# An up-projection by seven block products per tile, in fixed slots, behind two plain tiles

## The chip, the cores and the metric

The kernel runs on one core of one Trainium2 chip. Its time is the device time of one execution in microseconds (us). Before the change the median of three runs is 2341.06 us (2338.14 to 2341.59). The engines are TensorE (PE, with PEld for its weight loads), VectorE (DVE), ScalarE (ACT), GpSimd (POOL) and SyncE (SP, which issues the DMAs here).

## The reference

One layer of a hybrid backbone: a mixer (a recurrent branch and a state-space branch, merged), then a gated MLP with a 3x3 depthwise convolution on a 16 x 64 grid of 1024 tokens, each with its norm, modulation and residual. The change lies in the MLP, with D_MODEL 1024 and FFN_DIM 2816:

```python
def conv_ffn(h, w_up, conv_w, conv_b, w_down, rows, cols):
    u, v = jnp.split(h @ w_up, 2, axis=-1)
    u = dwconv2d(u, conv_w, conv_b, rows, cols)
    return (jax.nn.gelu(u) * v) @ w_down
...
        hx2 = modulate(rmsnorm(x, norm_ffn_w[l]), mx[3], mx[4])
        x = x + mx[5] * conv_ffn(hx2, ffn_w_up[l], ffn_conv_w[l], ffn_conv_b[l], ffn_w_down[l], rows, GRID_W)
```

## The kernel before

Activations lie with features on the 128 partitions and the 1024 tokens along the columns (T = 1024, half H = 512). Every fp32 product is done in three matmuls: an operand is split into a high part (ACT copies it to a rounded type) and a low part (DVE subtracts the copy), and `gdense` adds hi*hi, hi*lo and lo*hi over the K tiles of 128 features, 512 columns at a time, with `matmul` on line 124. Weights come by `wload`: a DMA into `raw` (512 KB), then the split into `whi`/`wlo`, with two of each, at high priority. The small helpers `stt`, `tt` and `act` (lines 156, 159, 162) issue all DVE and ACT work, so these three lines appear in most rows.

`tail` runs the MLP. `wout` writes the mixer's result into x1 (tiles M0 to M7) for the first and then the second half of the tokens. The norm of a half (`norm`, then `apply` per K tile: DVE scales, ACT writes the high part, DVE the low part, into tiles A0 to A15) is woven into what follows: the norm of the second half into the first up tile. Then `up` runs for f = 0 to 21. One tile f is 128 features of u and of v: 2 x 8 x 3 x 2 = 96 matmuls of 512 columns, u into a PSUM tile `d`, v into two PSUM tiles `s`. On u follow the convolution (ACT: centre tap and bias, `facc<-d,vec`; DVE: eight taps, `facc<-d,vec,facc`), the gelu on ACT, the product with v on DVE (`facc<-facc,s`), and the split into a pair of H tiles. After f = 7 and f = 14 `down` multiplies seven of these h tiles by the down weights, eight output tiles by two halves, and adds into x1; after f = 21 `last_down` does the last eight h tiles in pieces of 512, 256 and 256 tokens, with the final norm of a piece woven into the next one.

The order on each engine in this stage is left to the tile scheduler: by priority and readiness, with the program's order as its first guide. The tiles H, A, M, `raw` and `facc` rotate in pools, so a tile comes free when its last reader is done.

Of the kernel before, what the change touches and what calls it, by code (L numbers as in the profile page):

```python
# [45 lines left out]
class Builder:  # L46
    def __init__(self, nc, tc, A):
        self.nc, self.tc, self.A = nc, tc, A
        self.uid = 0
        self.wslot = 0  # L50
        self.groom = False
        self.turn = False
        self.wx = None
        self.st = getattr(nc, self.STORE)
# [100 lines left out]
    def stt(self, out, in0, s, in1, op0=ALU.mult, op1=ALU.add):  # L155
        self.nc.vector.scalar_tensor_tensor(out, in0, s, in1, op0=op0, op1=op1)  # L156

    def tt(self, out, a, b, op=ALU.mult):
        self.nc.vector.tensor_tensor(out, a, b, op=op)  # L159

    def act(self, out, in_, f, **kw):
        self.nc.scalar.activation(out, in_, f, **kw)  # L162
# [107 lines left out]
    def setup(self, cpool):  # L270
# [6 lines left out]
        self.mU = self.t(cpool, P, "mU")  # L277
        self.mL = self.t(cpool, P, "mL")
# [3 lines left out]
        nc.gpsimd.affine_select(out=self.mU, in_=self.ones, pattern=[[1, P]], compare_op=ALU.is_ge,  # L282
                                fill=0.0, base=0, channel_multiplier=-1)
        nc.gpsimd.affine_select(out=self.mL, in_=self.ones, pattern=[[-1, P]], compare_op=ALU.is_ge,
                                fill=0.0, base=0, channel_multiplier=1)
# [406 lines left out]
    def ssd(self):  # L692
# [429 lines left out]
    def up(self, f, x, split, parts):  # L1122
        A, p2, fh, fl = self.A, self.p2, x["fh"], x["fl"]
        pu = self.t(self.psD, T, "d")
        spans = [[(0, H)], [(H, T)]] if split else [self.FULL]
        wu = self.wload(A["wup"][f])
        if split:
            wv = self.wload(A["wup"][NF + f])
            pv = [self.t(self.psS, H, "s") for _ in range(2)]
            for sp in spans[:1]:  # L1130
                yield from self.gdense(pu, wu, fh, fl, sp)
                yield from self.gdense(pv, wv, fh, fl, sp)
            spans = spans[1:]
        for sp in spans:
            yield from self.gdense(pu, wu, fh, fl, sp)
        acc = self.t(p2, T, "facc")
        wc = [self.v("ffn_conv_w", tap * NF + f) for tap in range(9)]
        a3 = acc.rearrange("p (r c) -> p r c", c=64)
        u3 = pu.rearrange("p (r c) -> p r c", c=64)
        step = 16 // parts  # L1140
        for q in range(parts):
            lo, hi = q * step, q * step + step
            self.act(a3[:, lo:hi], u3[:, lo:hi], AF.Identity, bias=self.v("ffn_conv_b", f), scale=wc[4])
            for tap in (1, 7, 0, 2, 3, 5, 6, 8):
                dy, dx = tap // 3 - 1, tap % 3 - 1
                r0, r1 = max(lo, -dy), min(hi, 16 - max(0, dy))
                c0, c1 = max(0, -dx), 64 - max(0, dx)
                o = a3[:, r0:r1, c0:c1]
                self.stt(o, u3[:, r0 + dy : r1 + dy, c0 + dx : c1 + dx], wc[tap], o)
        if not split:  # L1150
            wv = self.wload(A["wup"][NF + f])
            pv = [self.t(self.psS, H, "s") for _ in range(2)]
        for sp in spans:
            yield from self.gdense(pv, wv, fh, fl, sp)
        i = f % 8
        h = self.t(self.pH, T, f"H{2 * i}", F32R)
        l = self.t(self.pH, T, f"H{2 * i + 1}", F32R)
        step = T // parts
        for q in range(parts):
            sl = slice(q * step, q * step + step)  # L1160
# [191 lines left out]
```

## Time and profile before

| | us |
|---|---|
| median of 3 runs | 2341.06 |
| the profiled execution | 2342.84 |
| its span, first to last instruction | 2341.1 |
| TensorE busy (matmuls) | 2285.2 (98%) |
| DVE busy | 1613.5 (69%) |
| ACT busy | 1061.3 (45%) |
| POOL busy | 2.4 (0%) |
| mean granted TensorE clock | 0.99 |

A row of the profile names line, engine and operation, then out<-in by the names that the program gives its tiles, shapes, and how many. "Idle before" tells how long the engine had stood still and what released it. The first up tile starts near 1604 us, the last one ends near 2235 us.

### The profile page before, as it was taken

How to read it: one execution, taken by the hardware profiler on the slowest of the kernel's cores; microseconds unless marked ns; L12 is line 12 of the kernel's file. 1: busy time of each engine (PE TensorE's matmuls, PEld its weight loads, DVE VectorE, ACT ScalarE, POOL GpSimd, SP SyncE). 2: the span in 40 equal slices, each digit the busy share in tenths (PEclk: the TensorE clock that was granted, in tenths of full speed). 3: DMA queues.
4: the chain of work that ended last, by engine and by line, in shares of the span. 5: the costliest groups of instructions: out<-in, count | busy, mean ns of one | idle time of the engine just before them, and what ended most of it. 6: DMA issues, size and time to landing. Idle time of an engine off the chain costs nothing.

```text
span 2341.1 us, 29454 instructions
## 1 busy us (share of the span) xinstructions
PE 2285.2 (98%) x11530; PEld 1896.3 (81%) x11530; DVE 1613.5 (69%) x2586; ACT 1061.3 (45%) x1596; POOL 2.4 (0%) x14
## 2 busy tenths in 40 slices
PE   7999999999999999999999999999999999999998
PEld 3778878778888888888888778888888888888888
DVE  4977877889978858758866675467764367436655
ACT  4477667677766556656635222333221122112231
POOL 0000000000000000000000000000000000000000
PEclk8999999999999999999999999999999999999999
DMA  6212222144434334424348765432111111111112
GB/s 253 95 62 73 95 84 70 59 129 149 133 124 149 120 102 142 145 77 150 114 136 271 233 220 187 154 97 63 54 44 48 53 45 52 42 51 54 46 54 73
DMA packets 81455, 251.78 MB, mean 108 GB/s; under 512 B 9731, under 2 KB 15907, under 8 KB 76069
## 3 DMA queue, kind: packets, MB, share of 16 engines
q1 hardware_dynamic: 81312, 249.90, 32.9%
q8 instruction: 90, 1.47, 0.3%
q14 instruction: 49, 0.39, 0.1%
q10 hardware_dynamic: 4, 0.01, 0.0%
HBM read 222.33 MB, written 27.54 MB: 107 GB/s over the span
## 4 chain that ended last, share of the span: by engine, by line
PE 84%; DVE 10%; DMA 3%; ACT 2%; issue 1%; DVEq 0%; ACTq 0%
PE d L124 42%; PE s L124 30%; PE s L985 2%; PE s L656 2%; PE s L977 1%; DVE wlo L159 1%; DVE L L159 1%; PE s L926 1%; DMA adar<-in_ada 1%; PE s L925 1%; ACT L L162 1%; PE s L314 1%; DVE L L681 1%; DMA raw<-in_w 1%; PE s L598 1%
## 5 line engine op out<-in xcount | busy, mean ns | idle before, releaser
L124 PE MATMUL d<-H,whi 128*128 128x512 f32 x2464 | 690.4, 398 | 0.4 <-ACT whi L162 0.2
L124 PEld LDWEIGHTS d<-H,whi 128*128 128x128 f32 x2464 | 451.0, 189 | 93.5 <-issue 6.0
L162 ACT ACTIVATE whi<-raw 128x1024 fp32r<-128x1024 f32 (+1 forms) x194 | 203.1, 1049 | 567.3 <-PE s L124 346.5
L124 PE MATMUL d<-H,wlo 128*128 128x512 f32 x1232 | 386.5, 393 | 2.0 <-DVE wlo L159 2.0
L159 DVE TENSOR_TENSOR wlo<-raw,whi 128x1024 fp32r<-128x1024 f32 (+1 forms) x194 | 234.4, 1210 | 188.7 <-ACT whi L162 187.2
L124 PEld LDWEIGHTS d<-H,wlo 128*128 128x128 f32 x1232 | 229.9, 188 | 51.5 <-DVE wlo L159 3.7
L124 PE MATMUL s<-A,whi 128*128 128x512 f32 x960 | 258.4, 389 | 0.0
L124 PE MATMUL d<-A,whi 128*128 128x512 f32 x960 | 258.3, 389 | 0.0
L124 PE MATMUL s<-H,whi 128*128 128x512 f32 x832 | 252.5, 391 | 2.7 <-ACT whi L162 2.7
L156 DVE SCALAR_TENSOR_TENSOR facc<-d,vec,facc 128x945 f32<-128x945 f32 (+5 forms) x184 | 216.8, 1178 | 11.2 <-ACT facc L162 5.9
L124 PEld LDWEIGHTS d<-A,whi 128*128 128x128 f32 x960 | 180.2, 188 | 37.6
L124 PEld LDWEIGHTS s<-A,whi 128*128 128x128 f32 x960 | 180.2, 188 | 37.3
L124 PEld LDWEIGHTS s<-H,whi 128*128 128x128 f32 x832 | 156.6, 189 | 36.0 <-ACT whi L162 3.1
L162 ACT ACT_TABLE_LOAD x102 | 130.9, 1283 | 84.3 <-DVE cacc L156 28.9
L156 DVE SCALAR_TENSOR_TENSOR M<-s,mods,M 128x512 f32<-128x512 f32 (+1 forms) x72 | 49.7, 691 | 160.4 <-PE s L124 160.2
L124 PE MATMUL s<-H,wlo 128*128 128x512 f32 x416 | 157.4, 391 | 1.4 <-DVE wlo L159 1.3
L124 PE MATMUL s<-A,wlo 128*128 128x512 f32 x480 | 149.2, 389 | 0.5 <-DVE wlo L159 0.5
L124 PE MATMUL d<-A,wlo 128*128 128x512 f32 x480 | 149.1, 389 | 0.0
L124 PEld LDWEIGHTS s<-A,wlo 128*128 128x128 f32 x480 | 90.0, 188 | 19.5 <-DVE wlo L159 1.0
L124 PEld LDWEIGHTS d<-A,wlo 128*128 128x128 f32 x480 | 90.1, 188 | 18.7
L156 DVE SCALAR_TENSOR_TENSOR E<-E,cst 128x128 f32<-128x128 f32 x256 | 82.3, 349 | 19.5 <-ACT E L162 19.5
L162 ACT ACTIVATE m<-GU,dtt 128x128 f32<-128x128 f32 x256 | 78.7, 389 | 35.0 <-PE s L977 29.8
(273 smaller groups left out, 3130.4 us busy)
## 6 DMA issues: line engine op xcount, KB each, us to landing
raw<-in_w SPq DMA_DIRECT2D x92, 512.0 KB, 3.6
E<-csd SPq DMA_DIRECT2D x32, 1024.0 KB, 6.7
raw<-in_wup SPq DMA_DIRECT2D x44, 512.0 KB, 3.6
R<-csd SPq DMA_DIRECT2D x64, 256.0 KB, 4.6
adar<-in_ada SPq DMA_DIRECT2D x32, 512.0 KB, 3.9
gated<-sg SPq DMA_DIRECT2D x32, 256.0 KB, 3.8
gd<-y SPq DMA_DIRECT2D x32, 256.0 KB, 2.3
gk<-gd SPq DMA_DIRECT2D x32, 256.0 KB, 5.6
```

The source lines that it names most:

```text
L124: nc.tensor.matmul(o, a[:, k, :], b[k][:, xo + s : xo + e], start=(k == 0 and i == 0), stop=(k == kn - 1 and i == 2))
L156: self.nc.vector.scalar_tensor_tensor(out, in0, s, in1, op0=op0, op1=op1)
L159: self.nc.vector.tensor_tensor(out, a, b, op=op)
L162: self.nc.scalar.activation(out, in_, f, **kw)
L314: self.nc.tensor.matmul(ps[:2, :], scc[:, k, :], w[:, k, :], start=(k == 0), stop=(k == 7))
L598: nc.tensor.matmul(pss, self.bt[j // 4][:, c, :], xw[:, c, :, :], start=(c == 0), stop=(c == 1))
L656: nc.tensor.matmul(pg, a[:, q, :], b[:, s:e], start=(i == 0), stop=(i == 2))
L681: nc.vector.tensor_tensor_scan(b1[:, L - 1 : TX - 1 : -1], a[:, L - 1 : TX - 1 : -1], b1[:, L - 1 : TX - 1 : -1], b1[:, 0:1], op0=ALU.mult ...
L925: nc.tensor.matmul(ps[:, s - s2, 0, :], btok[:, s, :], xw[:, 0, s, :], start=True, stop=True)
L926: nc.tensor.matmul(ps[:, s - s2, 1, :], btok[:, 7 - s, :], xw[:, 1, 7 - s, :], start=True, stop=True)
L977: nc.tensor.matmul(psy[q, c, :], self.xt[:, c0 + c, q], m[:, h, c, :], start=True, stop=True)
L985: nc.tensor.matmul(pso[:, c, :], S[:, cc if d == 0 else 7 - cc, d, :], CT[:, cc * P : (cc + 1) * P], start=True, stop=True)
```

## The change

Tiles f = 0 and 1 are kept plain (`up_plain`): the same 96 matmuls, written as eight products of a half of K by a half of the tokens. For f = 2 to 21 the tile is a 2 x 2 block product (K halves; u and v; token halves) that is done by a Winograd form with seven products instead of eight. The blocks of the activations are added and subtracted once (`blocks` during tiles 0 and 1: 24 DVE and 12 ACT operations; `blocks_late` in slots 2 to 9: the fourth block of product 22, 16 DVE and 4 ACT). The blocks of the weights are added per tile on POOL (`up_sum` and inside `up_split`, four per tile), and POOL also makes the low part of each of the seven weight blocks. Sums of products are formed in PSUM where the sign allows it, and three partial sums per tile are copied out by ACT and added back by DVE.

`ups` sets the order: one slot per product (4 K tiles x 3 = 12 matmuls), with the weight split three slots ahead, two taps of the previous tile's convolution per slot in four slots, the gelu in the next and the two gate products in the one after. All instructions of these slots are pinned to the program's order on every engine (`pin`). Product 22 of a tile is done one tile later, in the second slot. Since the A and H tiles hold the blocks, the gated h tiles are stored to DRAM (`h_d`) and loaded again (`hload`) for the down rounds, which now all run after the last up tile. The masks mU and mL are made later, when the state-space stage opens.

The instructions by engine: PE loses 240 matmuls of 128x512 and nothing else; DVE goes from 2588 to 2635 and ACT from 1600 to 1785; POOL gets 220 two-input operations of 128x512 and four of 128x1024; SP gets 22 stores to and 22 loads from `hd`. Ahead of the tail the order is the same on every engine, but for mU and mL on POOL.

```diff
 
     def stt(self, out, in0, s, in1, op0=ALU.mult, op1=ALU.add):
-        self.nc.vector.scalar_tensor_tensor(out, in0, s, in1, op0=op0, op1=op1)
+        self.pin(self.nc.vector.scalar_tensor_tensor(out, in0, s, in1, op0=op0, op1=op1))
...
-        self.mU = self.t(cpool, P, "mU")
-        self.mL = self.t(cpool, P, "mL")
...
+            self.mU = self.t(q1, P, "mU")
+            self.mL = self.t(q1, P, "mL")
...
+    PRODUCTS = ("11", "12", "s2", "s1", "s3", "s4", "22")
+    CLASSIC = 2
+    AHEAD_SPLIT = 3
+
+    def pin(self, ins):
+
+        return self.tc.keep_in_program_order(ins) if self.pinned else ins
+
+    def ptt(self, out, a, b, op):
+        self.pin(self.nc.gpsimd.tensor_tensor(out, a, b, op=op))
+
+    def up_plain(self, f, x, split):
+
...
+        for n, hf in ((0, 0), (1, 0), (0, 1), (1, 1)) if split else ((0, 0), (0, 1), (1, 0), (1, 1)):
...
+            yield from self.gdense(pv[hf] if n else pu[:, hf * H : hf * H + H], wv if n else wu, xh, xl, [(0, H)])
+            if (n, hf) == (0, 1):
+                for _ in self.conv2d(f, pu):
+                    pass
+                acc = self.convacc
+        self.act(acc, acc, AF.Gelu_apprx_tanh)
...
+    def up_sum(self, f, i, x):
+
+        u, v = x["raw"][f]
+        if i == 0:
+            q = self.t(self.wp, T, "raw")
+            a, b = x["sums"][f] = (q[:, :H], q[:, H:])
+            self.ptt(a, v[:, :H], v[:, H:], ALU.add)
+        else:
+            a, b = x["sums"][f]
+            self.ptt(b, a, u[:, :H], ALU.subtract)
+
+    def up_split(self, f, p, x):
...
+        self.pslot = (self.pslot + 1) % 4
+        w = self.t(self.wp, T, ("whi0", "wlo0", "whi1", "wlo1")[self.pslot], F32R)
+        hi, lo = w[:, :H], w[:, H:]
+        self.act(hi, src, AF.Copy)
+        self.ptt(lo, src, hi.bitcast(F32), ALU.subtract)
...
+    def up_product(self, f, p, x):
+
...
+        ps = st["z"] if p in ("s3", "22") else st["u"][:, :H] if p == "12" else st["u"][:, H:]
+        hi, lo = x["w"].pop((f, p))
+        for k in range(4):
+            bh, bl = x["b"][p][k]
+            for i, (a, b) in enumerate(((hi, bh), (hi, bl), (lo, bh))):
+                self.pin(self.nc.tensor.matmul(ps, a[:, k, :], b, start=(k == 0 and i == 0 and p in ("11", "12", "s3")),
+                                               stop=(k == 3 and i == 2), skip_group_check=True))
+        if p == "11":
+            st["s1"] = self.t(self.p1, H, "sql")
+            self.act(st["s1"], ps, AF.Copy)
+        elif p == "12":
+            self.tt(ps, ps, st["s1"], op=ALU.add)
+        elif p == "s2":
+            st["s2"] = self.t(self.p2, H, "ssq")
+            self.act(st["s2"], ps, AF.Copy)
+        elif p == "s1":
+            st["s4"] = self.t(self.p1, H, "s4") if f % 2 else self.t(self.gp, H, "sg")
+            self.act(st["s4"], ps, AF.Copy)
+        elif p == "s3":
+            self.tt(st["s4"], ps, st["s4"], op=ALU.add)
+        elif p == "22":
+            self.tt(st["s2"], ps, st["s2"], op=ALU.add)
+
+    def up_post(self, f, x):
+
+        st = x["st"][f]
+        yield from self.conv2d(f, st["u"])
+        acc = self.convacc
+        self.act(acc, acc, AF.Gelu_apprx_tanh)
+        yield
+        for i, v in ((1, st["s4"]), (0, st["s2"])):
+            self.tt(acc[:, i * H : i * H + H], acc[:, i * H : i * H + H], v)
+        yield
+        self.pin(self.st.dma_start(self.h_d[f], acc))
...
+    def ups(self, x, last):
+
+        C, n = self.CLASSIC, self.AHEAD_SPLIT
+        seq = [(C, p) for p in ("11", "12", "s2", "s1", "s3", "s4")]
+        seq += [(C + 1, "11"), (C + 1, "s2"), (C + 1, "12"), (C, "22")] + [(C + 1, p) for p in ("s1", "s3", "s4")]
+        for f in range(C + 2, NF):
+            seq += [(f, "11"), (f - 1, "22")] + [(f, p) for p in ("s2", "12", "s1", "s3", "s4")]
+        seq.append((NF - 1, "22"))
...
+        for i, (f, p) in enumerate(seq[: -n - 2]):
...
+            if q:
+                self.up_split(g, q, x)
...
+            for g in list(side):
+                if next(g, "end") == "end":
+                    side.remove(g)
+            next(last, None)
+            self.up_product(f, p, x)
...
+    def hload(self, f, x, raw=None, pool=False):
+        raw = self.t(self.p2, T, "facc") if raw is None else raw
+        self.pin(self.nc.sync.dma_start(raw, self.h_d[f]))
+        h, l = [self.room(x, q) for q in self.H_ROOM[f]]
+        self.act(h, raw, AF.Copy)
+        (self.ptt if pool else self.tt)(l, raw, h.bitcast(F32), ALU.subtract)
         x["h"][f] = (h, l)
...
+            def apply1(k, rs):
+
...
+                self.act(h, q, AF.Identity, bias=shift)
+                self.act(q, q, AF.Identity, bias=shift)
+                self.tt(l, q, h.bitcast(F32), op=ALU.subtract)
...
+                    self.tt(t1, b12, b11[k], op=ALU.subtract)
+                    self.tt(t2, b22, t1, op=ALU.subtract)
+                    part("s2", k, t2, f"H{4 + k}")
...
+                    self.tt(t3, b22, b12, op=ALU.subtract)
+                    part("s1", k, t1, f"A{(10, 11, 8, 9)[k]}")
...
+                    self.tt(a, bh, th, op=ALU.subtract)
+                    self.tt(a, a, bl, op=ALU.add)
+                    self.tt(a, a, tl, op=ALU.subtract)
+                    yield
+                    part("22", k, a, f"H{k}")
...
-            for f in range(NF):
-                self.weave(self.up(f, x, f == 0, 2 if f == NF - 1 else 1), side, self.RATIO[4])
-                side = None
-                if f in ends:
-                    self.down(ends[f], x)
+            self.weave(self.chain(*[self.up_plain(f, x, f == 0) for f in range(C)]), x["blocks"], self.RATIO[4])
+            self.ups(x, blocks_late())
+            for r in range(len(self.ROUNDS) - 1):
+                self.down(r, x)
```

On ACT, at a tile of before (f = 17; `whi` are weight copies, `facc<-d,vec` starts the convolution, `facc<-facc` is the gelu, H the high part of h):

```order
L162 ACTIVATE whi1_1985_14790<-raw_1984_14788 128x1024
L162 ACTIVATE facc_1975_14714<-d_1971_14659,vec_1_72 128x1024
L162 ACTIVATE whi0_1989_14854<-raw_1988_14852 128x1024
L162 ACTIVATE facc_1975_14714<-facc_1975_14714 128x1024
L162 ACTIVATE H2_1981_14780<-facc_1975_14714 128x1024
L162 ACTIVATE whi1_1997_14918<-raw_1996_14916 128x1024
```

On ACT, where the plain tiles pass to the slots (facc_1852 and facc_1866 are tiles 0 and 1; wlo0_1871 is the weight copy of the first new product, sql_1876 and ssq_1882 are its copies of partial sums out of PSUM tile d_1875; H7, A9 and H15 are blocks of the activations):

```order
L163 ACTIVATE H7_1857_13263<-ssq_1855_13259 128x512
L163 ACTIVATE H15_1859_13276<-sql_1856_13260 128x512
L163 ACT_TABLE_LOAD
L163 ACTIVATE facc_1852_13239<-facc_1852_13239 128x1024
L163 ACTIVATE wlo0_1871_13423<-A12_1801_13026 128x512
L163 ACTIVATE whi0_1874_13433<-raw_1870_13420 128x512
L163 ACTIVATE sql_1876_13450<-d_1875_13437 128x512
L163 ACTIVATE wlo0_1878_13454<-raw_1870_13420 128x512
L163 ACTIVATE whi1_1879_13470<-raw_1870_13420 128x512
L163 ACTIVATE facc_1866_13352<-facc_1866_13352 128x1024
L163 ACTIVATE ssq_1882_13491<-d_1875_13437 128x512
```

Weight copies that stood ahead of the gelu of the running tile now stand behind the gelu of the tile before, and a copy that TensorE's next product needs stands behind the gelu of tile 1.

On DVE, at the same tile of before (the taps, between two weight subtractions, the gate products and the low part of h):

```order
L159 TENSOR_TENSOR wlo1_1986_14791<-raw_1984_14788,whi1_1985_14790 128x1024
L156 SCALAR_TENSOR_TENSOR facc_1975_14714<-d_1971_14659,vec_1_72,facc_1975_14714 128x960 x2
L156 SCALAR_TENSOR_TENSOR facc_1975_14714<-d_1971_14659,vec_1_72,facc_1975_14714 128x15x63 x2
L156 SCALAR_TENSOR_TENSOR facc_1975_14714<-d_1971_14659,vec_1_72,facc_1975_14714 128x16x63 x2
L156 SCALAR_TENSOR_TENSOR facc_1975_14714<-d_1971_14659,vec_1_72,facc_1975_14714 128x15x63 x2
L159 TENSOR_TENSOR wlo0_1990_14855<-raw_1988_14852,whi0_1989_14854 128x1024
L159 TENSOR_TENSOR facc_1975_14714<-facc_1975_14714,s_1979_14730 128x512
L159 TENSOR_TENSOR facc_1975_14714<-facc_1975_14714,s_1980_14731 128x512
L159 TENSOR_TENSOR H3_1982_14781<-facc_1975_14714,H2_1981_14780 128x1024
```

On DVE, in the convolution of the first new tile (facc_1892, from its last s4_1893 on; s4_1893 and s4_1902 are the third and fourth block of product 22, H2 and H3 their low parts, d_1894 the sum of the next tile's product 12):

```order
L160 TENSOR_TENSOR s4_1893_13561<-s4_1893_13561,H6_1850_13229 128x512
L157 SCALAR_TENSOR_TENSOR facc_1892_13557<-d_1875_13437,vec_1_72,facc_1892_13557 128x15x63 x2
L160 TENSOR_TENSOR H2_1898_13588<-s4_1893_13561,H2_1898_13588 128x512
L157 SCALAR_TENSOR_TENSOR facc_1892_13557<-d_1875_13437,vec_1_72,facc_1892_13557 128x16x63 x2
L160 TENSOR_TENSOR s4_1902_13612<-A7_1701_12389,H7_1857_13263 128x512
L160 TENSOR_TENSOR s4_1902_13612<-s4_1902_13612,A7_1701_12389 128x512
L160 TENSOR_TENSOR s4_1902_13612<-s4_1902_13612,H7_1857_13263 128x512
L160 TENSOR_TENSOR d_1894_13565<-d_1894_13565,sql_1895_13578 128x512
L157 SCALAR_TENSOR_TENSOR facc_1892_13557<-d_1875_13437,vec_1_72,facc_1892_13557 128x15x63 x2
L160 TENSOR_TENSOR H3_1904_13634<-s4_1902_13612,H3_1904_13634 128x512
```

The taps, which stood in one piece, are now taken apart by pairs, and the last block preparations of product 22 lie between them: the low part H3 stands behind all eight taps.

## Rows read from the trace of the kernel before

**Rows 1.** The page, busy time by engine, and the granted clock by slice:

```profile
PE 2285.2 (98%) x11530; PEld 1896.3 (81%) x11530; DVE 1613.5 (69%) x2586; ACT 1061.3 (45%) x1596; POOL 2.4 (0%) x14
...
PEclk8999999999999999999999999999999999999999
```

**Rows 2.** The page, chain that ended last, shares by engine:

```profile
PE 84%; DVE 10%; DMA 3%; ACT 2%; issue 1%; DVEq 0%; ACTq 0%
```

**Rows 3.** That chain in order of time, 1590 to 2341 us (start, length, count):

```profile
1626.04 10.88 PE d L124 x48
1636.91 10.88 PE s L124 x48
...
2213.55 10.88 PE d L124 x48
```

**Rows 4.** Windows of 60 us: busy time and count by engine, clock, DMA share, GB/s:

```profile
1620.00:1680.00 60.00, 60.00 (x266) 49.63 (x265) 45.40 (x42) 18.64 (x18) 0.00 (x0) 1.00 0.17 53
...
1740.00:1800.00 60.00, 60.00 (x267) 49.69 (x266) 34.72 (x33) 12.38 (x12) 0.00 (x0) 1.00 0.13 39
1800.00:1860.00 60.00, 60.00 (x266) 49.71 (x265) 15.84 (x18) 5.95 (x6) 0.00 (x0) 1.00 0.19 58
```

**Rows 5.** TensorE's waits, 1600 us to the end (total, times, longest):

```profile
PE d L208 <- DVE frdg L207: 1.9, 1, 1.9
PE d L198 <- DVE sql L159: 0.9, 1, 0.9
```

**Rows 6.** DVE in order of time, 1990 to 2035 us (start, length):

```profile
1997.62 10.03 DVE L156 SCALAR_TENSOR_TENSOR facc<-d,vec,facc 128x960 f32<-128x960 f32 x8
...
2008.84 1.28 DVE L159 TENSOR_TENSOR facc<-facc,s 128x512 f32<-128x512 f32 x2 [0.19 <-ACT facc L162]
```

**Rows 7.** Groups by shape, 1626 to 2220 us (busy us, mean ns, idle before):

```profile
L159 DVE TENSOR_TENSOR wlo<-raw,whi 128x1024 fp32r<-128x1024 f32 x41 | 50.1, 1222 | 101.7 <-ACT whi L162 101.2
...
L159 DVE TENSOR_TENSOR facc<-facc,s 128x512 f32<-128x512 f32 x42 | 27.0, 684 | 3.7 <-ACT facc L162 2.7
...
L162 ACT ACTIVATE facc<-d,vec 128x1024 f32<-128x1024 f32 x20 | 23.9, 1193 | 0.0
L162 ACT ACTIVATE facc<-facc 128x1024 f32<-128x1024 f32 x21 | 22.3, 1064 | 12.7 <-DVE facc L156 12.7
```

**Rows 8.** ACT groups by shape, the whole trace:

```profile
L162 ACT ACT_TABLE_LOAD x102 | 130.9, 1283 | 84.3 <-DVE cacc L156 28.9 <-DVE xs L156 27.0 <-DVE bc L156 22.8
...
L162 ACT ACTIVATE sg<-d 128x512 f32<-128x512 f32 x32 | 18.8, 588 | 9.5 <-DMA gated<-sg 8.5 <-PE d L124 0.7
...
L162 ACT ACTIVATE sg<-sg 128x512 f32<-128x512 f32 x24 | 15.2, 632 | 81.2 <-DMA sg<-gated 81.2
...
L162 ACT ACTIVATE A<-facc,mods 128x512 fp32r<-128x512 f32 x16 | 11.1, 725 | 17.6 <-DVE facc L156 17.6
```

**Rows 9.** POOL in order of time, the whole trace:

```profile
0.81 0.20 POOL L279 MEMSET ones<- 128x128 f32 x1 [0.29 <-POOLq L1340]
1.08 0.29 POOL L280 TENSOR_SCALAR_AFFINE_SELECT ident<-ones 128x128 f32<-128x128 f32 x1
...
453.27 0.53 POOL L237 MEMSET btok<- 128x512 f32 x1 [364.82 <-DVE ge L159]
```

**Rows 10.** DVE in order of time, the second half's norm:

```profile
1610.56 1.41 DVE L156 SCALAR_TENSOR_TENSOR facc<-M,sc,d 128x512 f32<-128x512 f32 x2 [0.58 <-PE d L208]
...
1620.70 1.41 DVE L156 SCALAR_TENSOR_TENSOR A<-facc,mods,A 128x512 fp32r<-128x512 f32 x2
```

**Rows 11.** TensorE in order of time around a wait in the merge:

```profile
1337.00 0.61 PE L124 MATMUL d<-H,wlo 128*128 128x512 f32 x2
1340.31 2.08 PE L124 MATMUL s<-H,whi 128*128 128x512 f32 x4 [2.70 <-ACT whi L162]
1342.18 1.05 PE L124 MATMUL s<-H,wlo 128*128 128x512 f32 x2
```

**Rows 12.** Windows of 2 us there; the clock is the third number from the end:

```profile
1340.00:1342.00 2.00, 1.69 (x4) 1.26 (x5) 2.00 (x4) 0.26 (x1) 0.00 (x0) 0.50 0.83 176
1342.00:1344.00 2.00, 2.00 (x7) 1.67 (x7) 1.98 (x4) 0.00 (x0) 0.00 (x0) 0.68 1.00 364
```

**Rows 13.** The page, DMA issues: count, KB each, us to landing:

```profile
raw<-in_wup SPq DMA_DIRECT2D x44, 512.0 KB, 3.6
```

More of the change, by code (lines that the diff above doesn't have):

```diff
@@ L53, in __init__ @@
         self.wx = None
+        self.pinned = False
         self.st = getattr(nc, self.STORE)
@@ L1137, in up, with conv2d @@
+    def conv2d(self, f, ps):
+        acc = self.convacc = self.t(self.p2, T, "facc")
         wc = [self.v("ffn_conv_w", tap * NF + f) for tap in range(9)]
         a3 = acc.rearrange("p (r c) -> p r c", c=64)
[L1139 to L1160, printed above, removed]
-            self.act(acc[:, sl], acc[:, sl], AF.Gelu_apprx_tanh)
-            for i in range(2 * q // parts, 2 * (q + 1) // parts):
-                hs = slice(i * H, i * H + H)
-                self.tt(acc[:, hs], acc[:, hs], pv[i])
-            self.act(h[:, sl], acc[:, sl], AF.Copy)
-            self.tt(l[:, sl], acc[:, sl], h[:, sl].bitcast(F32), op=ALU.subtract)
+        u3 = ps.rearrange("p (r c) -> p r c", c=64)
@@ L1167, in up, with room @@
+    def room(self, x, tag, dt=F32R):
+        return self.t(x["pA"] if tag[0] == "A" else self.pH, T, tag, dt)
+    def hload(self, f, x, raw=None, pool=False):
[4 more added lines that the diff above has]
+        (self.ptt if pool else self.tt)(l, raw, h.bitcast(F32), ALU.subtract)
         x["h"][f] = (h, l)
-        yield
@@ L1175, in down @@
             w = self.wload(self.A[f"wd{r}"][m], kn * P, kn)
+            for g in list(x["side"]):
+                if next(g, "end") == "end":
+                    x["side"].remove(g)
+            if a + kn + m < self.ROUNDS[r + 1][1]:
+                self.hload(a + kn + m, x)
             for hf in range(2):
@@ new lines, in part, with blocks @@
+            def part(p, k, src, tag):
+                q = room(tag)
+                self.act(q[0], src, AF.Copy)
+                self.tt(q[1], src, q[0].bitcast(F32), op=ALU.subtract)
+                x["b"][p][k] = q
+            def blocks():
+                for k in range(4):
+                    b12, b22 = both[k]
+                    t1 = self.t(self.p2, H, "ssq")
+                    t2 = self.t(self.p2, H, "ssq")
+                    t3 = self.t(self.p1, H, "sql")
+                    self.tt(t1, b12, b11[k], op=ALU.subtract)
+                    self.tt(t2, b22, t1, op=ALU.subtract)
+                    part("s2", k, t2, f"H{4 + k}")
+                    yield
+                    self.tt(t3, b22, b12, op=ALU.subtract)
+                    part("s1", k, t1, f"A{(10, 11, 8, 9)[k]}")
+                    yield
+                    part("s3", k, t3, f"H{12 + k}")
+                    yield
```

155 lines of the change are left out of this document (120 added, 35 removed).

## The prediction

> **What bounds the kernel now.** I read the page first: TensorE is busy 2285.2 of 2341.1 us and its clock is at the upper of its two levels (2.4 GHz) in nearly every slice [rows 1]. The chain that ended last agrees: TensorE holds 84% of it, and "issue" 1% [rows 2]. So only what TensorE does, or what makes it wait, can move the end. The change sits in the last third, so next I read that chain in order of time from 1626 us on [rows 3]: the 39 runs of 48 matmuls that it lists from the second up tile on take 10.88 us each (two per tile, 21.76 us), and they follow each other and the down products without a gap. The 60 us windows say it again: TensorE 60.00 of 60.00 us at clock 1.00, VectorE (DVE) at most 45.4 us, ScalarE (ACT) under 19, GpSimd (POOL) nothing [rows 4]. Between 1600 us and the end TensorE's waits are 2.8 us in all, both in the final norms [rows 5]. The up stage is therefore pure matmul time: 10.88 / 48 = 0.2267 us per 128x512 matmul. A slot of the new schedule (one product, 12 matmuls) is 2.72 us, a tile of seven slots 19.04 us.
>
> **What the change removes.** The first two tiles keep their 96 matmuls. The other 20 have 7 x 12 = 84; the order of instructions confirms 240 fewer on TensorE and nothing else there. 240 x 0.2267 = **54.4 us** come off the bound, if TensorE goes on without waiting.
>
> **What it adds, steady state.** Per tile, DVE keeps eight taps (10.03 us in one run) and two gate products (1.28 the pair) [rows 6] and gets three adds of a PSUM partial, 0.69 each [rows 7]: 13.4 of 19.04 us. It loses the two weight subtractions (1.22 each [rows 7]), which go to POOL. ACT has seven 512-wide weight copies (0.63), three PSUM copies (0.59), the conv start (1.19) and the gelu (1.06): 8.4 us [rows 7, 8]. Both have room. What matters is order, since every engine is held to source order. A partial sum is copied out of PSUM before the next product is added to it, so three copies per tile stand between products; with another product placed between, each has about 1.8 us to spare (a slot of 2.72 less 0.59 and hand-over). The longest loop: after product s4 of tile f come a weight copy, conv start, eight taps, an add, the gelu, and behind the gelu on ACT the copy that s4 of tile f+1 needs. 0.63 + 1.19 + 10.03 + 0.69 + 1.06 + 0.59 is 14.2, some 14.9 with hand-overs, and TensorE gets there six slots (16.3 us) later. **Slack about 1.5 us a tile, so steady state costs 0**; what it costs when that cover goes is rival 1.
>
> **POOL.** It gets 11 subtractions or adds of 128x512 per tile. The trace of before shows no POOL operation with two inputs, only memsets and a one-input select [rows 9], so the price is bounded: not below the 512-wide memset, 0.53 us, and not above eight times the 128-wide select, 8 x 0.29 = 2.3 us. From 128 to 512 columns the memset grows by 0.33 us, 0.86 ns a column; the select has one read more than the memset of its width: 0.09 us on 128 columns, 0.7 ns a column. A second read at the same price gives 0.86 + 0.7 + 0.7 = 2.26 ns a column, and with 0.09 fixed **1.25 us**, which I take because it is built from the nearest rows. Eleven are 13.75 of 19.04 us: POOL keeps up. It stops doing so at 19.04 / 11 = 1.73 us.
>
> The Trainium skill, "GPSIMD Engine Reference", section 3.1, measures a two-input add of 2048 fp32 columns at 4497 ns on GpSimd, about twice VectorE's; a quarter of that is an estimate of 1.12 us here, 12.4 us a tile, and the sum would not move. Its section 4.1 advises VectorE for such work; no trace of before shows either.
>
> **What it adds, the seam.** Where the plain tiles hand over to the fixed slots, DVE and ACT are late. Call U the end of the second plain tile.
> (a) The norm of the second half now makes two ACT copies per block instead of one (0.725 each [rows 8]), so ACT sets its pace: about 0.8 us on the first plain tile. Before, that norm ran from 1610.56 to 1622.12 us [rows 10].
> (b) After it DVE must do, before U (1647.8 + 0.8), 21 block operations of 0.64, two weight subtractions of 1.22 and eight taps of 10.03 us: its last tap of tile 0 ends near U + 0.2. On ACT the weight copy of the first new product stands behind the table load (1.28) and the gelu (1.06) of tile 0, which waits for that tap (order of ACT in the section on the change). Copy done at U + 3.3, POOL's low half at U + 4.6, the product's other ten matmuls to U + 6.9 instead of 2.7: **4.2 us**.
> (c) The copy of partial s2 stands behind the gelu of tile 1, whose taps end near U + 11.5; gelu and copy: U + 13.5. TensorE would be there at 12.3: **1.2 us**.
> (d) In the next tile s2 follows 11 directly and waits for its copy: **0.9 us**.
> (e) The late product 22 of the first new tile needs its fourth block. s4 of this tile ends at U + 21.7, the conv start at 23.1 (order of DVE in the section on the change); then DVE does in order eight taps (10.03) and nine 512-wide operations (6.2) before that block's low half: U + 39.3. TensorE is at that matmul at 33.0: **6.3 us**. Sum of (b) to (e): 12.6, say 13.
> (f) Clock. When TensorE last stood idle 2.70 us, its next six matmuls took 2.73 us where 1.36 is usual [rows 11], and the granted clock read 0.50 and 0.68 in two windows of 2 us [rows 12], that is part at 1.2 GHz. The first product's wait and (e) are that long: 2 x 1.4 = **2.8 us**. Waits under 1 us leave the clock at 1.00.
> (g) DVE beside POOL. Eight of the nine operations in (e) read two SBUF tiles while POOL runs. If each waits for a whole POOL operation that is up to 8 x 1.3 = 10.6 us, if they do not disturb each other 0. With POOL busy three quarters of the time and half an operation left on average, **4 us**.
>
> The Trainium skill, "SBUF — State Buffer", section "Who interferes with whom", says that DVE and GpSimd share a port pair as an exclusive lock, and that a DVE operation with at most one SBUF input is not touched. By that the taps (PSUM and one SBUF tile) run free, and only (g) and the gates pay; no run here shows it yet.
>
> **The rest.** h tiles go to DRAM and come back: 22 stores and 22 loads of 512 KB. A load of this size lands 3.6 us after issue [rows 13] and the DMA engines are at 0.13 to 0.19 in this stage [rows 4]; the loads are issued a slot or more ahead: 0. At the boundary to the down rounds one low half on POOL (1024 wide, 2.5 us) comes late behind ACT's last weight copy: **1.5 us**. The two masks made on POOL ahead of the memset at 453.27 us: 0 to 0.6, taken as 0, since what follows is far ahead of TensorE.
>
> **Sum.** 54.4 - (0.8 + 13 + 2.8 + 4 + 1.5 = 22.1) = 32.3 us. The profiled run took 2342.84 us, 1.78 more than the median of 2341.06. 2342.84 - 32.3 = 2310.5; against the median **2309 us**.
>
> **Rivals.** 1: *the slack of 1.5 us goes.* If each of the eight taps takes 0.4 us more beside POOL, every loop is 3.2 us longer and TensorE waits 1.7 us in each of some 19 tiles: 32 us, and the time is 2341. It would be at or above the old time from there. For it: 1.5 us is thin. Against: each tap reads PSUM and one tile only, and its duration is the same 10.03 us in eight whatever ACT does.
> 2, on the other side: *POOL is the bound.* At the upper price, 2.3 us, a tile needs 25.3 us of POOL, 6.3 more than its slots; 20 tiles lose 126 us and the time is about 2435. It decides from 1.73 us on and eats the whole gain at about 1.88 (32.3 / 20 = 1.6 us per tile, over 11 operations 0.15 above 1.73). For it: no row shows this operation. Against: two reads priced from rows give 1.25.
> 3: *the seam is hidden*, because DVE catches up during the first plain tile. Then only (a), (g) and the boundary remain: 54.4 - 6.3 = 48.1, and 2293.
> That the change does not do what it says is excluded by the order.
>
> **Chances.** Forecast 0.70, rival 3 0.09, rival 1 0.12 (0.05 still faster, 0.04 level, 0.03 slower), rival 2 0.06, anything not thought of 0.03, slower. About 0.2% (4.7 us) is what can be told from no change. Faster 0.84, same 0.04, slower 0.12. The range: 2293 below, rival 3, also the seam without (f) and (g); above, (g) in full (+6.6), POOL at 1.6 us in (b) and at the boundary (+2), and 0.8 us in each of 19 tiles (+15): 2333.
>
> **What will show it.** TensorE's slots of 2.72 us in runs of tiles without waits; one wait of 3 to 5 us for the first split, one near 6 to 10 us before product 22 of the third tile, clock below 1.00 behind each; POOL operations near 1.25 us. If POOL shows 1.8 us or more, or TensorE waits in every tile for a copy on ACT, I am wrong.

## The result

The changed kernel takes 2364.99 us (median of 4 runs, 2359.47 to 2367.92) against 2341.32 us: 1.010 times the time before, 95% interval 1.0078 to 1.0123. It is 24 us slower where 32 us less were forecast, and lies outside the range of 2293 to 2333. One run of one kernel below (2485.57 us) had a lower granted clock throughout, 0.845 in the mean, and is left out.

Its page, busy time by engine, the slices of four engines, and the chain that ended last; compare [rows 1, 2]:

```profile
PE 2250.8 (95%) x11290; PEld 1851.0 (79%) x11290; DVE 1653.9 (70%) x2633; ACT 1148.2 (49%) x1781; POOL 306.2 (13%) x238
...
PE   7999999999999999999999999999799999989998
...
POOL 0000000000000000000000000002566666630000
PEclk7999999999999999999999999999899999999999
...
PE 67%; DVE 20%; DMA 6%; ACT 4%; issue 2%; POOLq 0%; SPq 0%; POOL 0%; DVEq 0%; ACTq 0%
```

TensorE has 240 matmuls less and is busy 34 us less, but its share of the chain fell from 84 to 67%, and DVE's rose from 10 to 20%. The stretch is the one with POOL in it. Windows of 60 us of the changed kernel, columns as in [rows 4]:

```profile
1620.00:1680.00 60.00, 48.95 (x192) 37.77 (x190) 50.69 (x54) 21.21 (x32) 27.91 (x19) 0.91 0.11 36
...
1800.00:1860.00 60.00, 55.16 (x238) 43.99 (x238) 38.23 (x36) 22.02 (x33) 40.87 (x31) 1.00 0.24 70
1860.00:1920.00 60.00, 54.47 (x234) 43.13 (x233) 38.28 (x37) 22.65 (x34) 40.17 (x32) 1.00 0.26 79
```

Before, TensorE had 60.00 of 60.00 us there [rows 4]. Now it stands idle 4.8 and 5.5 us in the last two windows, with DVE at 38 and POOL at 40 to 41 of 60: no engine is full. So it is a wait. TensorE's waits from 1590 us to the end, where [rows 5] had two:

```profile
PE d L1217 <- DVE d L160: 25.6, 19, 3.6
PE d L1217 <- ACT ssq L163: 16.0, 20, 3.0
PE d L1217 <- ACT wlo L163: 3.1, 1, 3.1
PE s L1217 <- ACT H L163: 2.8, 1, 2.8
PE s L1217 <- DVE H L160: 2.4, 1, 2.4
```

Two waits come in every tile: 19 times for DVE's add into PSUM tile d, 20 times for ACT's copy of s2's partial sum. One tile on TensorE, in order of time; the products are s1, s3, s4 of one tile, then 11, the late 22, s2 and 12 of the next, and again s1:

```profile
1866.53 3.06 PE L1217 MATMUL d<-A,wlo 128*128 128x512 f32 x12 [1.16 <-DVE d L160]
1869.42 2.88 PE L1217 MATMUL s<-H,whi 128*128 128x512 f32 x12
1872.14 2.88 PE L1217 MATMUL d<-H,wlo 128*128 128x512 f32 x12
1874.86 2.88 PE L1217 MATMUL d<-A,whi 128*128 128x512 f32 x12
1877.58 2.88 PE L1217 MATMUL s<-H,wlo 128*128 128x512 f32 x12
1880.30 2.88 PE L1217 MATMUL d<-H,whi 128*128 128x512 f32 x12
1883.87 3.01 PE L1217 MATMUL d<-A,wlo 128*128 128x512 f32 x12 [0.69 <-ACT ssq L163]
1888.04 3.04 PE L1217 MATMUL d<-A,whi 128*128 128x512 f32 x12 [1.16 <-DVE d L160]
```

Slots are 2.72 us apart as forecast, but product 12 starts 0.85 us late and s1 some 1.4 us. From 1716.15 to 2059.85 us 16 tiles pass: 21.48 us each instead of 19.04, hardly less than the 21.76 of before. What s1 waits for is DVE's add of that tile; here is DVE in the same tile:

```profile
1876.88 4.95 DVE L157 SCALAR_TENSOR_TENSOR facc<-d,vec,facc 128x960 f32<-128x960 f32 x4 [3.78 <-ACT facc L163]
1881.74 0.68 DVE L160 TENSOR_TENSOR ssq<-s,ssq 128x512 f32<-128x512 f32 x1
1882.34 5.04 DVE L157 SCALAR_TENSOR_TENSOR facc<-d,vec,facc 128x1008 f32<-128x1008 f32 x4
1887.30 0.69 DVE L160 TENSOR_TENSOR d<-d,sql 128x512 f32<-128x512 f32 x1
1888.58 0.93 DVE L160 TENSOR_TENSOR facc<-facc,s 128x512 f32<-128x512 f32 x1 [0.59 <-ACT facc L163]
```

The add of the new tile (d<-d,sql) stands behind the eight taps of the tile before. The loop that ends there closes so (estimate from these rows): s1 (3.06), s3 and s4 (5.45), weight copy and conv start on ACT (1.8), taps with one add between (10.4), the add (0.70), and s1 of the next tile: 21.4 us.

The books from the place where the second plain tile hands over (the next matmul would start there without a wait): before, 2341.1 - 1647.63 = 693.5 us to the end of the span, now 2357.8 - 1641.48 = 716.3, that is 22.8 more where 54.4 less were due: 77.2 us of losses. The first 13 slots, which I call the seam (35.4 us of matmuls), took 61.55 until 1703.03: 26.2 too many. The 18 tiles after it took 389.6 instead of 342.7: 46.9. The passage to the down rounds and the rest hold the last 4.1. The profiled run reached the plain tiles 6 us sooner than the run of before; it is also 5.5 us below its own median.

### The profile page after: what moved, and what is told of

The parts are those of the page before. It is cut to its first block, busy times and chain, and to the rows that moved or that the text cites. A ratio compares the mean times of both kernels' runs of the same rounds, so it can differ in the third digit from the quotient of the medians.

```text
span 2357.8 us, 29730 instructions
## 1 busy us (share of the span) xinstructions
PE 2250.8 (95%) x11290; PEld 1851.0 (79%) x11290; DVE 1653.9 (70%) x2633; ACT 1148.2 (49%) x1781; POOL 306.2 (13%) x238
## 3 DMA queue, kind: packets, MB, share of 16 engines
q8 instruction: 89, 1.46, 0.3%
## 4 chain that ended last, share of the span: by engine, by line
PE 67%; DVE 20%; DMA 6%; ACT 4%; issue 2%; POOLq 0%; SPq 0%; POOL 0%; DVEq 0%; ACTq 0%
PE d L125 29%; PE s L125 18%; DVE facc L157 8%; PE d L1217 6%; DMA adar<-in_ada 3%; PE s L1217 2%; PE s L986 2%; PE s L651 2%; DVE wlo L160 2%; ACT L L163 1%; PE s L978 1%; DVE L L160 1%; PE s L927 1%; DMA gk<-gd 1%; PE s L926 1%
## 5 line engine op out<-in xcount | busy, mean ns | idle before, releaser
L163 ACT ACTIVATE whi<-raw 128x1024 fp32r<-128x1024 f32 (+2 forms) x194 | 185.8, 959 | 268.1 <-PE s L125 115.3
L157 DVE SCALAR_TENSOR_TENSOR facc<-d,vec,facc 128x945 f32<-128x945 f32 (+2 forms) x176 | 214.8, 1220 | 74.3 <-ACT facc L163 70.0
L160 DVE TENSOR_TENSOR wlo<-raw,whi 128x1024 fp32r<-128x1024 f32 (+1 forms) x154 | 186.5, 1213 | 78.7 <-ACT whi L163 77.4
L125 PE MATMUL s<-H,whi 128*128 128x512 f32 x672 | 202.5, 390 | 0.4 <-ACT whi L163 0.4
L125 PE MATMUL s<-A,whi 128*128 128x512 f32 x480 | 138.3, 390 | 1.9 <-POOL A L1133 1.0
L1217 PE MATMUL d<-A,wlo 128*128 128x512 f32 x372 | 97.0, 411 | 24.6 <-DVE d L160 11.7
L1217 PEld LDWEIGHTS d<-A,wlo 128*128 128x128 f32 x372 | 71.8, 198 | 48.3 <-DVE d L160 15.5
L125 PEld LDWEIGHTS s<-A,whi 128*128 128x128 f32 x480 | 90.1, 188 | 21.6 <-POOL A L1133 1.4
L1217 PE MATMUL d<-A,whi 128*128 128x512 f32 x348 | 86.3, 397 | 17.9 <-DVE d L160 10.3
L1217 PEld LDWEIGHTS d<-A,whi 128*128 128x128 f32 x348 | 63.8, 188 | 39.3 <-DVE d L160 14.1
L157 DVE SCALAR_TENSOR_TENSOR m<-GL,dtt,m 128x128 f32<-128x128 f32 x256 | 77.9, 348 | 20.7 <-ACT m L163 20.6
```

Of the source, the lines that this page charges most:

```text
L125: nc.tensor.matmul(o, a[:, k, :], b[k][:, xo + s : xo + e], start=(k == 0 and i == 0), stop=(k == kn - 1 and i == 2))
L157: self.pin(self.nc.vector.scalar_tensor_tensor(out, in0, s, in1, op0=op0, op1=op1))
L160: self.pin(self.nc.vector.tensor_tensor(out, a, b, op=op))
L163: self.pin(self.nc.scalar.activation(out, in_, f, **kw))
L1217: self.pin(self.nc.tensor.matmul(ps, a[:, k, :], b, start=(k == 0 and i == 0 and p in ("11", "12", "s3")), stop=(k == 3 and i == 2), skip_ ...
```

## The experiments

The theory after this reading is called the **shared tile**. Product 12 fills the first half of PSUM tile d, while s2 and s1 add into the second half. By the data they have nothing to do with each other, but the program tracks tile d as one. So product 12 waits until ACT has read the other half, and s1 waits until DVE has written the half that it doesn't touch. The rivals are the **gelu loop**, whose slack the prediction had worked out, and **POOL** holding DVE up.

**Both waits away.** Product 12 gets its own PSUM tile, and the add is issued behind s4; no engine has more or less to do.

```diff
+        if p == "12":
+            st["p"] = self.t(self.psS, H, "s")
-        ps = st["z"] if p in ("s3", "22") else st["u"][:, :H] if p == "12" else st["u"][:, H:]
+        ps = st["z"] if p in ("s3", "22") else st["p"] if p == "12" else st["u"][:, H:]
...
-        elif p == "12":
-            self.tt(ps, ps, st["s1"], op=ALU.add)
...
+        elif p == "s4":
+            self.tt(st["u"][:, :H], st["p"], st["s1"], op=ALU.add)
```

> Edit: product 12 gets a PSUM tile of its own, and DVE's add that forms the first half of u in tile d is issued behind product s4 instead of behind product 12. Same work on every engine. Theory (shared tile): in the changed kernel TensorE's product s1 waits in every tile for DVE's add into tile d, which stands behind eight taps, and product 12 waits for ACT's copy out of the other half of d; so a tile takes 21.47 us instead of 19.04. With both waits gone a tile is 19.04 us: 18 x 2.43 = 44 us less, 2321, and perhaps some us more at the seam, where the same two waits stand. Rival (gelu loop): the loop over the gelu and the copy behind it sets the tile's length; the edit leaves it, 2365. Rival (POOL): DVE is slowed by POOL beside it; the edit leaves that too, 2365.

Measured: 2308.57 us (2307.56 to 2309.11), 0.9858 of before, interval 0.9841 to 0.9874. That is 56 us less than the changed kernel. A window of it:

```profile
1800.00:1860.00 60.00, 60.00 (x266) 49.67 (x266) 42.74 (x42) 24.40 (x37) 45.99 (x35) 1.00 0.26 80
```

TensorE is full again, with more work per window on DVE and POOL than in the changed kernel. Both rivals foretold 2365 and fall. From the hand-over on, the two traces differ by 55 us: 46.9 in the 18 tiles (342.7 instead of 389.6; the 44, and 2.9 more, since in the last of them s1 waited 2.47 us for the add and then took 4.54), 5.9 in the seam, where the same two waits stood (55.67 us, 1645.32 to 1700.99, instead of 61.55), and 2.3 behind them.

**Only the add later.** Product 12 stays in tile d.

```diff
-        elif p == "12":
-            self.tt(ps, ps, st["s1"], op=ALU.add)
...
+        elif p == "s4":
+            self.tt(st["u"][:, :H], st["u"][:, :H], st["s1"], op=ALU.add)
```

> Edit: only the add is issued later, behind product s4; product 12 stays in tile d. Shared tile: the wait for the add goes, the wait of product 12 for the copy (0.69 and some 0.15 of restart) stays: a tile near 19.9 us, 18 x 1.6 = 28 us less, 2337. Both rivals: 2365.

Measured: 2328.32 us (2325.55 to 2330.82). The waits in its slots:

```profile
1735.84 3.01 PE L1217 MATMUL d<-A,whi 128*128 128x512 f32 x12 [0.69 <-ACT ssq L163]
...
1755.86 3.01 PE L1217 MATMUL d<-A,wlo 128*128 128x512 f32 x12 [0.69 <-ACT ssq L163]
```

20.02 us a tile: the wait for the add is gone, the wait for the copy costs 0.98 us per tile. 9 us better than expected; the expected sum held nothing for the seam, which took 55.9 us here instead of 61.6.

**Only the own PSUM tile.** The add stays behind product 12.

```diff
-            self.tt(ps, ps, st["s1"], op=ALU.add)
+            self.tt(st["u"][:, :H], ps, st["s1"], op=ALU.add)
```

> Edit: only product 12 gets its own PSUM tile; the add into d stays where it was. Shared tile: the 0.69 us wait per tile goes, but the loop over taps and add is as long as before, so s1 waits the longer: 21.47 us a tile, 2365 within 3. Rival (the copies): if the short waits for copies are a cost of their own, 18 x 0.85 = 15 us less, 2350.

Measured: 2378.93 us (2376.28 to 2380.18), 14 us slower than the changed kernel. The copy's wait is gone, and as the theory says nothing is won by it. But that it would cost was foretold by nobody. Its s1 product in three tiles:

```profile
1718.69 4.61 PE L1219 MATMUL d<-A,whi 128*128 128x512 f32 x12 [2.08 <-DVE d L160]
1741.80 3.06 PE L1219 MATMUL d<-A,wlo 128*128 128x512 f32 x12 [2.14 <-DVE d L160]
1763.31 4.61 PE L1219 MATMUL d<-A,whi 128*128 128x512 f32 x12 [2.14 <-DVE d L160]
```

One idle stretch of 2.1 us stands where 0.69 and 1.16 stood. In 9 of the 16 tiles from 1718.69 to 2055.48 us, mostly every second one, the product behind it takes 4.2 to 4.6 us instead of 3.0, and the tile 23.1 us instead of 21.5: 9 x 1.6 = 14 us, about the loss. Windows of 2 us of this kernel behind the first two of these stretches show the clock, columns as in [rows 12]:

```profile
1718.00:1720.00 2.00, 1.31 (x5) 1.11 (x6) 1.42 (x3) 1.06 (x1) 1.92 (x2) 0.92 0.00 0
1720.00:1722.00 2.00, 2.00 (x6) 1.52 (x6) 1.07 (x2) 0.00 (x0) 0.00 (x0) 0.50 0.00 0
1722.00:1724.00 2.00, 2.00 (x8) 1.60 (x7) 0.00 (x0) 0.67 (x2) 0.00 (x0) 0.73 0.00 0
...
1742.00:1744.00 2.00, 2.00 (x9) 1.59 (x9) 1.68 (x2) 0.29 (x1) 0.97 (x1) 1.00 0.00 0
```

In the changed kernel the clock read 1.00 in the 60 us windows from 1740 to 2040 us.

**POOL's work on DVE.** On top of the kernel with both waits gone.

```diff
-        self.pin(self.nc.gpsimd.tensor_tensor(out, a, b, op=op))
+        self.pin(self.nc.vector.tensor_tensor(out, a, b, op=op))
```

> Edit: on top of the kernel with both waits gone, the 11 operations per tile that POOL does are done by DVE; POOL does nothing in the up stage. DVE then has 10.03 + 2.1 + 1.4 + 11 x 0.64 = 20.5 us per tile against 19.04: if DVE is the bound, 1.5 us or more in each of 18 tiles, 27 us more and further delays of weights behind the taps: 2335 to 2360. If POOL's longer operations and its holding up of DVE cost more than that: below 2308.

Measured: 2350.34 us (2344.36 to 2355.7), 1.0041 of before. TensorE's waits and a window:

```profile
PE d L1219 <- ACT s L163: 15.7, 9, 1.9
PE d L1219 <- ACT sg L163: 10.8, 9, 1.9
...
1860.00:1920.00 60.00, 54.22 (x230) 43.73 (x229) 55.06 (x70) 20.95 (x33) 0.00 (x0) 0.97 0.23 77
```

Here the gelu loop appears: s4 waits up to 1.9 us in a tile (26.5 us over 18 tiles) for the copy of s1's partial (s or sg), which stands behind the gelu on ACT, and the gelu behind taps that share DVE with 11 more operations. The tile from 1872.40 to 1893.67 takes 21.27 us. So that loop is real and its slack is thin, but in the changed kernel it was not the one that ended last. It also prices POOL: with it the kernel is 42 us faster, though POOL's operation takes 1.29 us and DVE's 0.69.

**The seam.** Most of what is left of the losses lies there: 55.7 us for 35.4 of matmuls. First both the weights and the block preparation earlier, then the weights alone, on top of the kernel with both waits gone:

```diff
-        self.pslot = 0
+        self.pslot = 1
...
             next(last, None)
+            next(last, None)
             self.up_product(f, p, x)
```

> Edit: the first kernel of this list, with the seam changed too: the first new weight block goes to the ring's place that comes free half a plain tile earlier, and the preparation of product 22 takes two steps per slot instead of one. Shared tile and seam as read from the trace of the changed kernel (first product 5.8 us late, product 22 of the first new tile 5.2 us of waits and 1.8 us of slow clock): 8 to 13 us less than the first kernel of this list, near 2308. If the seam's waits only move to the next operation that DVE is late with: within 3 us of the first kernel of this list.

Measured: 2309.37 us (2308.46 to 2311.65): the same. The wait moved:

```profile
PE d L1219 <- ACT ssq L163: 13.3, 1, 13.3
```

The copy of s2's partial now stands on ACT behind two copies of blocks that wait for DVE, and s1 waits 13.3 us for it.

> Edit: on top of the kernel with both waits gone, only the ring of split weights starts one place later, so that the first product's weights can be split before the second plain tile ends. Theory (weights at the seam cost by themselves): the waits of 3.1 and 0.6 us and the slow clock behind them go, 4 to 5 us less: 2304. Theory (DVE is late at the seam, and sets its end): the first product starts earlier, but the later waits for what DVE and ACT still have to do grow by as much: 2308 within 2.

Measured (only the first of the two edits): 2308.85 us (2306.86 to 2309.95): the same. The first product no longer waits for its weights (3.1 and 0.6 us before), and TensorE waits elsewhere:

```profile
PE s L1219 <- ACT H L163: 4.5, 1, 4.5
PE s L1219 <- DVE H L160: 2.8, 2, 1.5
PE d L1219 <- ACT sg L163: 2.1, 1, 2.1
PE s L1219 <- DVE s L160: 2.1, 1, 2.1
```

The waits for the blocks of product 22 (H) are as without the edit (4.5 and 2.7), and the one for sg grew from 0.6. The last one does not lie in the seam: it is the late product 22 of the last tile, at 2046.25 us. The seam became 2.1 us shorter (53.6 us), and what lies behind the 18 tiles 1.5 longer. So the second theory has the time right, but not all of the mechanism: the weights did cost 2 us in the seam, half of what the first theory gave them, and the rest of their wait moved on. What remains there is mostly waits for blocks that DVE prepares. Can DVE be relieved by POOL, which is nearly idle during the plain tiles?

```diff
-                self.tt(q[1], src, q[0].bitcast(F32), op=ALU.subtract)
+                (self.tt if p == "22" else self.ptt)(q[1], src, q[0].bitcast(F32), ALU.subtract)
```

> Edit: on top of the kernel with both waits gone, the 12 low parts of the blocks made during the plain tiles go from DVE to POOL, 12 x 0.64 = 7.7 us of DVE. DVE is late at the seam: 3 to 7 us less, 2304; less of it if POOL and DVE hold each other up there (DVE's own two-input operations took 1.66 instead of 0.69 us beside POOL), down to nothing. Weights at the seam alone: 2308.

Measured: 2312.34 us (median of three runs, 2312.29 to 2316.41), 4 us slower than without the edit.

> Edit: both edits together, the ring one place later and the 12 low parts on POOL. DVE is late: TensorE and DVE both get ahead, 5 to 10 us less than with both waits gone alone: 2301. Weights alone: as with the ring edit alone.

Measured: 2312.59 us (2311.22 to 2317.55), 4 us slower. A wait in a plain tile is new:

```profile
PE d L125 <- DVE wlo L160: 4.0, 1, 4.0
```

The weights of a plain tile, split by DVE, come late. Ahead of that split DVE now waits twice for a low part that POOL makes (1.19 and 1.18 us), and two of its operations take 1.76 and 1.74 us beside POOL instead of 0.68 (below). That this is the reason for all of the 4 us was not shown by a run of its own.

Three plain tiles instead of two (and the two buffers of s1's partial in turn from there), then with both seam edits:

```diff
-    CLASSIC = 2
+    CLASSIC = 3
...
-            st["s4"] = self.t(self.p1, H, "s4") if f % 2 else self.t(self.gp, H, "sg")
+            st["s4"] = self.t(self.p1, H, "s4") if (f - self.CLASSIC) % 2 else self.t(self.gp, H, "sg")
```

> Edit: on top of the kernel with both waits gone, three plain tiles instead of two. TensorE has 12 matmuls, 2.7 us, more; DVE gets a tile of 21.8 us with some 12.5 us of work to catch up before the slots. If the seam costs what it does (some 17 us of waits and slow clock) because DVE is late when the slots begin, half of it or more goes: 2308.6 + 2.7 - 9 = 2302. If the seam's cost is in the slots themselves (product 22 of the first new tile waits for blocks that are prepared between taps anyway): 2311.

Measured: 2309.45 us (2304.49 to 2310.41). The same as with two plain tiles, and a miss of the first expectation: the waits ahead of product 22 shrank, but its own stayed, with rows like those of two plain tiles (4.46 us for H3's high part, 1.12 and 1.49 for low parts). So three plain tiles give DVE time, and pay 2.7 us of TensorE for it, but the preparation between the taps is as late as before. The seam took 51.7 us, 4.0 less than with two plain tiles; beside the 2.7, a wait of 2.1 us at the last product 22 (for sg) eats it up.

> Edit: three plain tiles, the ring of split weights one place later, and two steps of block preparation per slot. If DVE is in time at the seam, the preparation can now be done ahead of the taps: 4 to 8 us less than with three plain tiles alone, 2296. If the preparation on DVE only delays the copies on ACT behind it, as with two plain tiles: equal within 2.

Measured: 2305.71 us (2303.83 to 2307.48), 4 us less than three plain tiles alone, the lower end of the first expectation (its 2296 was not reached); the intervals (0.9836 to 0.9865 of before, and 0.9841 to 0.9881) overlap, but the seam in the traces is shorter too, 48.3 us. s1 still waits 9.4 us once, for the same copy as with two plain tiles and two steps per slot.

Last, the preparation of product 22 from the first slot on, one step per slot: with three plain tiles and the ring edit, and with two plain tiles alone.

```diff
             def blocks_late():
 
-                for _ in range(2):
-                    yield
                 for k in range(4):
```

> Edit: three plain tiles, the ring one place later, and the block preparation for product 22 begins in the first slot instead of the third, one step per slot as before. With three plain tiles alone the waits for that preparation were 7.1 us and the slow clock behind them 1.3. Two slots earlier is 5.4 us: if the preparation's place between the taps is what remains of the seam's cost, 4 to 8 us less than with three plain tiles alone, 2303. If an earlier preparation only holds up the copies on ACT (as with two steps per slot): equal within 2, 2309.

Measured: 2300.89 us (2298.72 to 2303.39), 0.9828 of before, interval 0.9811 to 0.9844: the best kernel here, 40 us faster than before and 64 faster than the changed one. Its seam took 45.5 us. How much of the 8.6 us against three plain tiles alone belongs to the ring edit was not measured.

> Edit: two plain tiles as in the changed kernel, both waits gone, and the block preparation for product 22 begins in the first slot. DVE still has the taps of the second plain tile then: the preparation can't begin before they end, so little is gained and the copies on ACT behind it wait: 2308 within 3. If the place between the taps is all that counts: 2303.

Measured: 2303.86 us (2301.07 to 2306.94), 0.9844 of before: 4.7 us less than without the edit. The intervals overlap, but all four runs lie below the four without it, and the seam took 51.5 us instead of 55.7, so my first theory for it fell. TensorE's waits in it:

```profile
PE d L1219 <- ACT ssq L163: 3.9, 1, 3.9
PE d L1219 <- ACT wlo L163: 3.1, 1, 3.1
PE d L1219 <- ACT sql L163: 1.9, 1, 1.9
...
PE s L1219 <- DVE H L160: 0.6, 1, 0.6
```

The waits of product 22 (7.2 us with both waits gone) are down to 0.6, and 3.9 came back at s1. What stays is split between weights, copies and blocks; no single cause is left.

## Why the prediction was wrong

**What bounds, and what comes off: right.** 240 matmuls less, slots of 2.72 us, 54.4 us. Where nothing waits, TensorE does a tile in 19.04 us.

**Steady state: wrong, and this is the step that failed.** The prediction set it at 0, because each PSUM copy had "another product placed between" it and the next product, and because it took the loop over gelu and copy for the longest. Both sentences followed data, not waits. Product 12 is no cover for the copy of s2 when both lie in one tile, and the add behind the taps is a release for s1. The price was 18 x 2.44 = 44 us, shown by taking the two waits away; the outcome belongs to the 0.03 of "anything not thought of". It could have been seen before any run: the order of the changed kernel with its waits, in every tile, reads at the first matmul of s1 (A10_1839 is a block of s1)

```
L1217 MATMUL d_1978_14272<-A10_1839_13188,whi1_1980_14287 128x512 [waits DVE_49]
```

and at s1 no operand had come from DVE for a long time. The DVE operation it waits for is the add, which writes the first 512 columns of d_1978; the matmul writes the last 512. With that loop in the sum the time would have been 2309 + 44 = 2353, to which 6 us of the same waits at the seam come: near 2360, against 2365. The prediction's sign for being wrong, a wait in every tile, was right; the loop it named for it (rival 1) was not: taps beside POOL took what they took before. DVE's groups of the changed kernel from 1703 to 2090 us (busy us, mean ns):

```profile
L157 DVE SCALAR_TENSOR_TENSOR facc<-d,vec,facc 128x945 f32<-128x945 f32 x72 | 86.5, 1202 | 2.5
...
L160 DVE TENSOR_TENSOR facc<-facc,ssq 128x512 f32<-128x512 f32 x17 | 30.2, 1776 | 0.0
L160 DVE TENSOR_TENSOR d<-d,sql 128x512 f32<-128x512 f32 x18 | 12.4, 689 | 0.0
...
L160 DVE TENSOR_TENSOR facc<-facc,sg 128x512 f32<-128x512 f32 x9 | 10.3, 1148 | 4.8 <-ACT facc L163 4.8
L160 DVE TENSOR_TENSOR facc<-facc,s 128x512 f32<-128x512 f32 x9 | 8.4, 933 | 5.4 <-ACT facc L163 5.4
```

Eight taps are still 10.0 us [rows 6], and one of the first row's taps takes 1202 ns here and 1198 in the run without POOL. Only the gate products, whose inputs both lie in SBUF now, are longer: 0.93 and 1.15 us the first (its v lies in a buffer s4, shown as s, or sg), 1.78 the second, where 0.68 was usual [rows 7]. In the loop above they stand behind the add that s1 waits for.

**POOL's price: right.** 1.29 us undisturbed, forecast 1.25. Rival 2 is out. The estimate from the Trainium skill, "GPSIMD Engine Reference", section 3.1, was 1.12: low by 0.17. Its section 4.1 advises VectorE for such work; the run with POOL's work on DVE was 42 us slower, since what counts here is which engine has room.

**(a): wrong, but small.** From the norm's first operation to the hand-over it took 37.1 us (1604.39 to 1641.48), before 37.1 too (1610.56 [rows 10] to 1647.63): 0, not 0.8.

**(b) to (g), the seam: the chain right, the size low.** The prediction had 19.8 us with clock and POOL; it took 26.2. The first product waited 3.1 for the copy and 0.6 for POOL, as described in (b), but ended 8.5 us after U instead of 6.9, part of it slow clock (10 matmuls in 3.9 us). Three waits of the shared tile were missing: 0.69 at product 12, 3.60 at s2, which found the clock low and took 5.49 us, and 2.98 at product 12 of the second new tile, for the copy of s2's partial. (e) to (g), product 22 and the slow clock behind it, took 7.9 us where 11.7 were forecast; the nine operations of (g) grew by 2.7 us beside POOL, not by 4 (and 8 x 1.3 is 10.4, not 10.6). With both waits gone the seam lost 55.7 - 35.4 = 20.3 us.

**(g) and the page on SBUF.** Beside POOL, DVE's operations with two SBUF inputs took up to 1.67 us in that preparation where 0.69 is usual, and the second gate product 1.78 in the mean. By the Trainium skill, "SBUF — State Buffer", section "Who interferes with whom", such operations contend with a GpSimd instruction that reads SBUF, and those with at most one SBUF input, outside the two-port modes, do not. The traces agree: the taps, with one input in PSUM, did not change, and DVE's adds from PSUM stayed at 0.68 to 0.69. In the run with POOL's work on DVE the second gate product is back at 0.69:

```profile
L160 DVE TENSOR_TENSOR facc<-facc,ssq 128x512 f32<-128x512 f32 x9 | 6.2, 685 | 0.0
```

**The rest.** The boundary cost 1.46 (22 of the last tile waits for DVE) and 1.8 us (first down matmuls, for DVE and POOL) instead of 1.5. Stores and loads of h showed no wait of their own on TensorE.

The kernel with both waits gone measured 2308.6 where the sum, which held nothing for them, said 2309. So the rest of the sum was of the right size. That it agrees within 1 us is luck: in the changed kernel single terms were off by 1 to 4 us, in both directions.

## What to carry to other kernels

Before calling a copy hidden, look at what each instruction waits for, not at what it needs: a tile that two engines use in halves is waited for as a whole, and an in-order engine passes on the wait of whatever stands ahead of the releasing instruction. In a schedule that repeats, write down every loop that leads from one round back to itself and compare it with the round's length; the longest one sets the pace, and a single add issued behind eight taps was worth 37 us here. Where a late engine set the end of a passage, pulling work forward mostly moved the wait (13.3 us at a copy queued behind it, in one run); it helped where the work began earlier and left the copies behind it less held up (3.9 us).

## What the hardware showed that I had not expected

The split of an idle time matters, not only its sum. Idle stretches of 0.69 and 1.16 us per tile left the granted clock at 1.00; one of 2.1 us in their place was followed by a low clock in 9 of 16 tiles (0.50 and 0.73 in windows of 2 us behind the stretch of 2.08), and made each such tile 1.6 us longer. Behind the next stretch, 2.14 us, the clock read 1.00, so its length alone does not decide; what does is not shown. All of them are shorter than the 2.70 us on which the prediction's price of a slow clock rested [rows 11, 12].

DVE and POOL delay each other in both directions. In the changed kernel these two stand side by side:

```profile
1867.92 1.78 DVE L160 TENSOR_TENSOR facc<-facc,ssq 128x512 f32<-128x512 f32 x1
...
1867.40 1.76 POOL L1133 TENSOR_TENSOR raw<-A 128x512 f32<-128x512 f32 x1
```

Without the other beside them they take 0.69 us (above) and 1.29.
